# Two sets of operand sums moved beside an mLSTM head, half a plain tile put inside the last head, and weights split one half ahead

## The chip, the cores and the metric

The kernel runs on one core of a Trainium2 chip. The metric is the device time of one execution in microseconds. The median of three timed runs of the kernel before is 2468.99 us (2468.9 to 2470.32).

## The reference

One inference step of a hybrid layer: an in-projection, an mLSTM branch and a sliding-window attention branch side by side, two branch projections that are gated and added, an out-projection and a layer norm. The prompt has 512 tokens, the decode batch 8 x 4 = 32 samples; the model width is 2048.

```python
q_m, k_m, v_m, o_m, z_m, q_a, k_a, v_a, z_a, g_m, g_a, i_pre, f_pre = parts   # of x @ w_in
# prompt and samples, with their own states:
h_m, C, n, m = _mlstm(q, k, v, ig, lf, C0, n0, m0)       # 4 heads of 512
h_a = _sink_attend(q, k, v, dist, valid, slopes, sinks)  # window of 128, 32 heads of 64
# merge:
br_m = hn.reshape(B, T, M_WIDTH) * jax.nn.sigmoid(o_m) * jax.nn.silu(z_m)
br_a = h_a * jax.nn.silu(z_a)
y = (jax.nn.sigmoid(g_m) * jnp.einsum('btc,cd->btd', br_m, w_proj_m)
     + jax.nn.sigmoid(g_a) * jnp.einsum('btc,cd->btd', br_a, w_proj_a))
out = jnp.einsum('btc,cd->btd', y, w_out)
return _layernorm(DN_ALPHA * x + out, ln_w, ln_b).astype(x.dtype)
```

## The kernel before

All activations are held transposed: 128 channels on the partitions, the 544 tokens (512 of the prompt, 32 samples) as columns, in two halves of 272. Column 240 on, up to 272, is called the rim in the code of the sample attention.

Every fp32 value is split into a high and a low part (`split` for weights, `hilo` for activations), and a product is three matmuls: high with high, high with low, low with high. Half a weight tile is 128 x 8 x 128 values (`raw`); ScalarE casts it to `wh` (L208), VectorE forms `wl` (L209), TensorE multiplies (L218 for a plain tile, L693 and L695 for paired ones). A plain tile is two halves of 48 matmuls of 272 columns. Pairs of tiles are computed with seven half products instead of eight, from sums of the operand's four quarters, called s1, n2, n3 and s4: four VectorE operations on a row k and row k + 8 together, and a high and a low part of each.

The program runs in stages on TensorE: the in-projection in pairs, up to about 1760 us, with the prompt's attention, the sample attention (about 890 to 1011 us) and the samples' mLSTM worked in between the products; then the prompt's four mLSTM heads (1765 to 1984 us) with plain tiles of w_proj_a (numbers 0 to 5) worked in between; plain tiles 6 and 7 and the pairs of w_proj_a; plain tiles 14 and 15; four plain tiles of w_proj_m (2085 to 2134 us), its pairs, w_out, and the layer norm.

A scheduler sets the order of each engine. The code gives it generators that are advanced between products (`spawn`, `tick`, `yield`), priorities (`high_priority`), and pins (`issue_after(x)`: not ahead of instruction x). Each engine and each DMA queue takes its instructions strictly in the order so set. SP's queue carries most loads and stores, POOL's the loads of tile `tx`.

Names that the change touches:

- `d_bra[k]` is row k of the attention branch, 128 x 544. `attention` stores `hT` into it when head pair k is done; from row 8 on it loaded row k - 8 into `s`, formed the sums (`branch_sums`) and stored them in `d_sa[k - 8]`.
- `sample_attention` leaves the samples' columns in `gas`, stores them to `d_bra`, loads the rim of all rows into a part of `kb` (the tile of the samples' keys), formed the sums of the rim there and stored them in `d_ss`. The samples' mLSTM follows on SP's queue: loads of its state `C`, its `qs`, `ks`, `vs`; then `kA`, `qcl` go through memory (`d_kv`) and come back as `KB` and `VB`.
- `mlstm` runs the prompt's heads: `values`, `keys`, then `cells` (four cells c a head; L1485 is the key cell's matmul, L1533 the last group of matmuls of a cell).
- `plain_a(ct, ...)` is a plain tile of w_proj_a; its evacuation to `c` is L1694.
- `operand_sums(src, to, p)` loads rows k and k + 8 into `tx` (two buffers in this stage), forms the sums and splits them; row k + 2 is loaded when the sums of row k are done.
- `gemm` is a plain tile of two halves; `merged` evacuates a tile of w_proj_m (L1759) and adds the gated other half (L1760).

Of the kernel before, what the change touches and what calls it, by code (L numbers as in the profile page):

```python
# [74 lines left out]
def _build(tc, nc, i, o, es):  # L75
# [154 lines left out]
        return [bank(), bank()]  # L230

    def gemm(wv, c0, xh, xl, cols=EVEN, raws=(None, None), every=8, prio=0, before=None, parts=(1, 1),
             ps=None, behind=None):
        ps = ps or mm()
        for half in range(2):
            if before:
                before(half)
            raw = raws[half] or load_half(wv, c0, half)
            if prio:
                with tc.high_priority(offset=prio):  # L240
                    wh, wl = split(raw, parts=parts[half])
            else:
                with tc.issue_after(behind.ins) if behind and half == 0 else ExitStack():
                    wh, wl = split(raw, parts=parts[half])
            products(ps, half, wh, wl, xh, xl, cols, every[half] if isinstance(every, tuple) else every)
        return ps

    def halves(ps, ap, r=ALL):
# [541 lines left out]
    def attention(k, qs, sz, kv):  # L790


        k1, k2, VA = kv
        hT = btile("b1", [128, SEQ], "hT")
        st = []
        for a in range(2):
            nb = btile("b1", [128, 256], "nb")
            A.activation(nb[:], state["ca"][:, 0:256], AF.Copy, scale=SLOPES[2 * k + a])
            s_ = scores_tile()
            mx, mn, sums = (btile("bm", [128, 4], t_) for t_ in ("mx", "mn", "sums"))  # L800
            h = slice(2 * k + a, 2 * k + a + 1)
# [12 lines left out]
        yield  # L814
        for a in range(2):
            s_, mx, mn, sums, h = st[a]
            for j in range(4):
                sj = s_[:, j, 128 if j == 0 else 0:256]
                A.activation(sj, sj, AF.Exp, bias=mn[:, j:j + 1], scale=-1.0, accum_out=sums[:, j:j + 1])
            G.tensor_tensor(out=s_[:, 1:4, 128:256], in0=s_[:, 1:4, 0:128], in1=s_[:, 1:4, 128:256], op=ALU.add)  # L820
            A.activation(mx[:], mn[:], AF.Exp, bias=sinkb[:, h])
            V.tensor_tensor(out=sums[:], in0=sums[:], in1=mx[:], op=ALU.add)
            V.reciprocal(sums[:], sums[:])
            for j in range(4):
                sj = s_[:, j, 128:256]
                A.activation(sj, sj, AF.Copy, scale=sums[:, j:j + 1])
            yield
        yield
        ps_ = []
        for a in range(2):  # L830
            s_ = st[a][0]
            pt = sm()
            for b in range(4):
                PE.transpose(pt[:, b * 128:b * 128 + 128], s_[:, b, 128:256], ident)  # L834
            fh, fl = s_[:, :, 0:128], s_[:, :, 128:256]
            A.copy(fh.bitcast(F32R), blk(pt[:]))
            V.tensor_tensor(out=fl.bitcast(F32R), in0=blk(pt[:]), in1=fh, op=ALU.subtract)
# [12 lines left out]
        if k > 7:  # L850
            sc = scores_tile()
            nc.sync.dma_start(sc[:, 0:4:2, 0:PC], d_bra[k - 8].rearrange("p (c x) -> p c x", c=2)[:, :, 0:PC])
        for a in range(2):
            yield
            po = sm()
            for b in range(4):
                n = 256 if b < 3 else 128
                for m, p_ in enumerate(ps_[a]):
                    PE.matmul(po[:, b * 128:b * 128 + n], VA[:, b], p_[:, 2 * b:2 * b + n // 128],  # L859
                              start=(b == 0 and m == 0), stop=(b == 3 and m == 1), skip_group_check=True)  # L860
            rows_ = slice(a * 64, a * 64 + 64)
# [6 lines left out]
        if k > 7:  # L868
            spawn(branch_sums(sc[:, :, 0:PC], hT[:, 0:PC], hT[:, HT:SEQ], d_sa[k - 8]))

    PC = SEQ - HT

    def branch_sums(t_, r12, r22, to):
        r11, s1, r21, s4 = (t_[:, j] for j in range(4))
# [3 lines left out]
        V.tensor_tensor(out=s4, in0=r12, in1=r11, op=ALU.subtract)  # L878
        nc.sync.dma_start(to, t_)
        yield  # L880

    waiting = {}
    state.update(open=False, done=0, samples=False)
# [71 lines left out]
    def sample_attention():  # L955
# [119 lines left out]
        left = kb[:].rearrange("p b x -> p (b x)")  # L1075
        rim = left[:, 1024:1536].rearrange("p (k t) -> p k t", k=16)
        with tc.issue_after(state["load"].ins):
            nc.sync.dma_start(rim, d_bra[:, :, PC:HT].rearrange("k p t -> p k t"))
        PTs = weightsT(0)
        before = iter(())  # L1080
        for b2_ in range(4):
# [7 lines left out]
        for _ in before:  # L1089
            yield  # L1090
        nc.sync.dma_start(d_bra[:, :, SEQ:T].rearrange("k p t -> p k t"), gas[:])
        t_ = left[:, 0:1024].rearrange("p (j k t) -> p j k t", j=4, k=8)
        V.tensor_copy(t_[:, 0], rim[:, 0:8])
        V.tensor_copy(t_[:, 2], gas[:, 0:8])
        for _ in branch_sums(t_, rim[:, 8:16], gas[:, 8:16], d_ss):
            pass

    def layernorm_rows(n, den, em, parts, hn, w):

# [369 lines left out]
    def keys(h, c, kt):  # L1469
# [12 lines left out]
        for b in range(4):  # L1482
            for n, (a, b_) in enumerate(((kwh, vh), (kwh, vl), (kwl, vh))):
                for f, pp in enumerate((p0, p1)):
                    state["cells"] = PE.matmul(pp[:, 0:258], a[:, b * 128:b * 128 + 128], b_[:, b, f],  # L1485
                              start=(b == 0 and n == 0), stop=(b == 3 and n == 2))
        co = f5()
        A.copy(co[:, 0:256], p0[:, 0:256])
        A.copy(co[:, 256:512], p1[:, 0:256])
# [70 lines left out]
    def mlstm():  # L1560
# [3 lines left out]
        pre["k"] = load4(d_k, 0)  # L1564
        yield
        for h in range(MH):
            vts, kts = pre["v"], pre["k"]
            state["head"] = state["pow"]
            spawn(decays(h))
# [41 lines left out]

    wm, wa_, wo = kview("w_proj_m"), kview("w_proj_a"), kview("w_out")
    spawn(mlstm())
    def operand_sums(src, to, p, far=2):

        def load(k):
            t_ = tx.tile([128, 2, T], F32, tag="tx", name=nm("tx"))
# [4 lines left out]
        for k in range(8):  # L1622
# [4 lines left out]
            V.tensor_tensor(out=r22, in0=r22, in1=r21, op=ALU.subtract)  # L1627
            V.scalar_tensor_tensor(r21, r11, -1.0, r21, op0=ALU.mult, op1=ALU.subtract)
            V.tensor_tensor(out=r11, in0=r11, in1=r22, op=ALU.subtract)
            V.tensor_tensor(out=r12, in0=r12, in1=r11, op=ALU.subtract)  # L1630
            for name, r_ in (("s1", r22), ("n2", r11), ("n3", r21), ("s4", r12)):
                if name not in to:
                    to[name] = quad(p, name)
                hilo(r_, to[name][0][:, k], to[name][1][:, k])
            if k + far < 8:
                ahead.append(load(k + far))

# [93 lines left out]
    next(sums_)  # L1731
    spawn(sums_)
    for ct in range(LEAD_A, PAIR_A):
        with tc.issue_after(state["cells"].ins):
            plain_a(ct, every=2, prio=AHEAD)
    esPS.close()
    psB, psA = psum_pools(4)
    XA = operands((bah_, bal_), SA)
# [24 lines left out]


    M = {}
    spawn(operand_sums(d_brm, M, act))
    for ct in range(4):
        merge = merged(ct, plain=True)
        sg = merge([p_[:, :HT] for p_ in gemm(wm, ct * 128, bmh, bml, every=4, prio=AHEAD)])
        nc.sync.dma_start(d_y[ct], sg[:])  # L1770
    drain()
    XM = operands(bm_, M)

# [349 lines left out]
```

## Time and profile before

| what | value |
|---|---|
| median of the timed runs | 2468.99 us |
| time of the profiled execution | 2472.84 us |
| its span, first to last instruction | 2471.1 us |
| mean granted TensorE clock | 0.996 |
| TensorE (PE) busy | 2443.2 us, 99% |
| VectorE (DVE) busy | 1903.9 us, 77% |
| ScalarE (ACT) busy | 1247.9 us, 50% |
| GpSimd (POOL) busy | 523.2 us, 21% |

A row of a group or of the timeline names the line of the kernel, the engine, the operation, the tiles (written, then read), and the shape. In the timeline the first two numbers are start and length in us, and the bracket at the end is the idle time of the engine just ahead and what ended it. In a window's row stand its length, then busy time and number of instructions of PE, PE's weight loads, DVE, ACT and POOL, then the granted clock, the mean share of the DMA engines and GB/s. SPq and POOLq are the DMA-issuing queues of SP and POOL.

### The profile page before, as it was taken

The page shows a single profiled execution, that of the slowest core. Times are in us where ns is not written, and L with a number is a line of the kernel's source. Part 1 is how long each engine was busy: PE and PEld are TensorE (multiplying, and loading weights), DVE is VectorE, ACT ScalarE, POOL GpSimd, SP SyncE. Part 2 cuts the span into 40 slices and gives each one's busy share as a digit, 9 for nine tenths or more (in the row PEclk, how much of TensorE's full clock was granted, in tenths as well). Part 3 has the DMA queues.
Part 4 walks back from the last instruction along what each step waited for, and adds up shares of the span by engine and source line. Part 5 has one row for each costly group of instructions (what it writes and reads, how often), then busy time and mean ns, then how long its engine had stood idle before and what let it go on. Part 6 is the DMA issues. An engine that isn't in the chain of part 4 may idle for free.

```text
span 2471.1 us, 48979 instructions
## 1 busy us (share of the span) xinstructions
PE 2443.2 (99%) x19394; PEld 2379.0 (96%) x19394; DVE 1903.9 (77%) x2857; ACT 1247.9 (50%) x2069; POOL 523.2 (21%) x504
## 2 busy tenths in 40 slices
PE   9999999999999999999999999999999999999999
PEld 8999999999999998989999999999999999999997
DVE  7768888888888887877877888777855676777656
ACT  6466676676676654433433444444644444434431
POOL 4114334333334320211111121211000120111111
PEclk9999999999999999999999999999999999999999
DMA  6876666666776754577687676676754598788776
GB/s 180 201 176 159 156 160 148 161 161 165 172 181 165 174 155 120 157 218 226 194 251 233 174 237 209 192 233 214 245 162 156 183 254 259 217 228 268 203 221 186
DMA packets 566846, 479.03 MB, mean 194 GB/s; under 512 B 46424, under 2 KB 461704, under 8 KB 566360
## 3 DMA queue, kind: packets, MB, share of 16 engines
q1 hardware_dynamic: 547864, 410.09, 56.2%
q0 software_dynamic: 17840, 64.23, 13.3%
q8 instruction: 153, 2.51, 0.4%
q10 hardware_dynamic: 912, 1.57, 0.2%
q14 instruction: 77, 0.63, 0.1%
HBM read 325.75 MB, written 100.77 MB: 173 GB/s over the span
## 4 chain that ended last, share of the span: by engine, by line
PE 91%; issue 3%; DMA 3%; DVE 2%; ACT 0%; SPq 0%; POOL 0%; ACTq 0%; DVEq 0%; POOLq 0%
PE bank L693 46%; PE bank L695 23%; PE bank L218 8%; PE sm L1485 2%; PE sm L218 1%; PE sm L1517 1%; PE sm L808 1%; PE bank L1292 1%; PE sm L1533 1%; PE sm L859 1%; DVE wl L209 1%; PE sm L1944 1%; PE sm L1297 1%; DMA VB<-d_kv 1%; PE sm L834 1%
## 5 line engine op out<-in xcount | busy, mean ns | idle before, releaser
L208 ACT CAST wh<-raw 128x1024 fp32r<-128x1024 f32 x641 | 671.5, 1048 | 834.7 <-PE bank L693 707.6
L209 DVE TENSOR_TENSOR wl<-raw,wh 128x1024 fp32r<-128x1024 f32 x641 | 801.1, 1251 | 204.8 <-ACT wh L208 183.3
L693 PE MATMUL bank<-xk,wh 128*128 128x272 f32 x2336 | 323.7, 289 | 0.2 <-ACT wh L208 0.2
L673 DVE TENSOR_TENSOR raw<-raw,raw 128x1024 f32<-128x1024 f32 x244 | 309.9, 1271 | 7.8 <-issue 2.5
L693 PEld LDWEIGHTS bank<-xk,wh 128*128 128x128 f32 x2336 | 303.2, 188 | 2.4 <-issue 1.5
L712 POOL TENSOR_TENSOR ev<-p,ev 128x272 f32<-128x272 f32 x85 | 114.3, 1345 | 461.6 <-ACT ev L711 419.3
L693 PE MATMUL bank<-n3h,wh 128*128 128x272 f32 x656 | 170.7, 292 | 1.0 <-ACT ev L716 0.6
L693 PE MATMUL bank<-n2h,wh 128*128 128x272 f32 x656 | 170.0, 291 | 0.0
L693 PE MATMUL bank<-s1h,wh 128*128 128x272 f32 x656 | 169.8, 291 | 0.0
L695 PE MATMUL bank<-xk,wl 128*128 128x272 f32 x1168 | 169.5, 287 | 0.0
L693 PE MATMUL bank<-n3l,wh 128*128 128x272 f32 x656 | 168.9, 289 | 0.0
L693 PE MATMUL bank<-n2l,wh 128*128 128x272 f32 x656 | 167.9, 287 | 0.0
L693 PE MATMUL bank<-s4h,wh 128*128 128x272 f32 x656 | 167.5, 289 | 0.0
L693 PE MATMUL bank<-s1l,wh 128*128 128x272 f32 x656 | 167.4, 287 | 0.0
L693 PE MATMUL bank<-s4l,wh 128*128 128x272 f32 x656 | 167.0, 287 | 0.0
L695 PEld LDWEIGHTS bank<-xk,wl 128*128 128x128 f32 x1168 | 155.5, 188 | 0.1
L671 POOL DMA_DIRECT2D raw<-raw x96 | 83.5, 870 | 323.9 <-DVE ev L720 209.5
L693 PE MATMUL bank<-a11h,wh 128*128 128x272 f32 x584 | 150.4, 289 | 0.0
L693 PE MATMUL bank<-a11l,wh 128*128 128x272 f32 x584 | 149.6, 288 | 0.0
L693 PEld LDWEIGHTS bank<-n3h,wh 128*128 128x128 f32 x656 | 124.5, 190 | 2.8 <-issue 1.5
L693 PEld LDWEIGHTS bank<-s1h,wh 128*128 128x128 f32 x656 | 123.2, 188 | 1.6 <-issue 1.0
L693 PEld LDWEIGHTS bank<-n2h,wh 128*128 128x128 f32 x656 | 123.3, 188 | 1.5 <-issue 1.4
(529 smaller groups left out, 5806.6 us busy)
## 6 DMA issues: line engine op xcount, KB each, us to landing
raw<-in_w_in SPq DMA_DIRECT2D x296, 512.0 KB
raw<-raw POOLq DMA_DIRECT2D x96, 512.0 KB, 5.1
C<-in_state_mlstm_C SPq DMA_DIRECT2D x32, 1024.0 KB
out<-C SPq DMA_DIRECT2D x64, 512.0 KB
raw<-in_w_proj_a SPq DMA_DIRECT2D x32, 512.0 KB
raw<-in_w_proj_m SPq DMA_DIRECT2D x32, 512.0 KB
raw<-in_w_out SPq DMA_DIRECT2D x32, 512.0 KB
d_v<-ev SPq DMA_DIRECT2D x16, 272.0 KB
```

The source lines that it names most:

```text
L208: state["cast"] = A.copy(wh[:, k:k + n], raw[:, k:k + n])
L209: state["split"] = V.tensor_tensor(out=wl[:, k:k + n], in0=raw[:, k:k + n], in1=r32(wh[:, k:k + n]), op=ALU.subtract)
L218: PE.matmul(ps[f][:, :w], a[:, kk], b(k, c, w), start=(k == 0 and n == 0), stop=(k == 15 and n == 2))
L671: G.dma_start(out=w[out][:], in_=w[b][:], accum_op=ALU.add)
L673: V.tensor_tensor(out=w[out][:], in0=w[a][:], in1=w[b][:], op=ALU.add)
L693: PE.matmul(ps, wh[:, k], x(p, k), start=(first and k == 0 and p == 0), stop=False, skip_group_check=True)
L695: state["end"] = PE.matmul(ps, wl[:, k], x(0, k), start=False, stop=(k == 7), skip_group_check=True)
L712: G.tensor_tensor(out=c22, in0=p1, in1=c11, op=ALU.subtract)
L808: PE.matmul(pp[:, c0 + w0:c0 + 256], qs[a][:, j * 128:j * 128 + 128], kx[:, k0:k0 + 256 - w0], start=(n == 0), stop=(n == 1))
L834: PE.transpose(pt[:, b * 128:b * 128 + 128], s_[:, b, 128:256], ident)
L859: PE.matmul(po[:, b * 128:b * 128 + n], VA[:, b], p_[:, 2 * b:2 * b + n // 128], start=(b == 0 and m == 0), stop=(b == 3 and m == 1), skip ...
L1485: state["cells"] = PE.matmul(pp[:, 0:258], a[:, b * 128:b * 128 + 128], b_[:, b, f], start=(b == 0 and n == 0), stop=(b == 3 and n == 2))
```

## The change

Four things are changed.

1. Row 15 of the attention branch no longer forms the sums with row 7, and the sample attention no longer forms those of the rim. A new generator, `last_sums`, does both. It is spawned at the start of the second head: it loads rows 7 and 15 and then the two rims, forms four sums each, and stores them in eight pieces.
2. The first half of plain tile 6 is pinned behind the key cell of c = 1 of the last head, and no longer behind that head's last cell.
3. The four plain tiles of w_proj_m are made by `lead`, which loads and splits the weights of the next half ahead of the products of this one.
4. The operand sums of that stage are pinned behind the last split and the last cast that stand ahead of them in the code.

The four lines of the sums are now a function, `four_sums` (L875 to L878).

```diff
-        if k > 7:
+        if 7 < k < 15:
             spawn(branch_sums(sc[:, :, 0:PC], hT[:, 0:PC], hT[:, HT:SEQ], d_sa[k - 8]))
+    def last_sums():
+        def store(pairs):
+            with tc.issue_after(state["load"].ins):
+                for to, src in pairs:
+                    nc.sync.dma_start(to, src)
+        p_, q_ = ev(), ev()
+        with tc.issue_after(state["load"].ins):
+            for t_, k in ((p_, 7), (q_, 15)):
+                nc.sync.dma_start(t_[:, 0:SEQ], d_bra[k][:, 0:SEQ])
+        for _ in range(4):
+            yield
+        (r11, r21), (r12, r22) = ((t_[:, 0:PC], t_[:, HT:SEQ]) for t_ in (p_, q_))
+        with tc.issue_after(state["split"].ins):
+            four_sums(r11, r12, r21, r22, r22, r12)
+        yield
+        store([(d_sa[7][:, j], r_) for j, r_ in enumerate((r11, r22, r21, r12))])
+        a_, b_ = (ev()[:, 0:16 * NS].rearrange("p (k t) -> p k t", k=16) for _ in range(2))
...
+        with tc.issue_after(state["split"].ins):
+            four_sums(r11, r12, r21, r22, r22, r12)
+        yield
+        store([(d_ss[:, j], r_) for j, r_ in enumerate((r11, r22, r21, r12))])
...
-        with tc.issue_after(state["load"].ins):
-            nc.sync.dma_start(rim, d_bra[:, :, PC:HT].rearrange("k p t -> p k t"))
...
-        for _ in branch_sums(t_, rim[:, 8:16], gas[:, 8:16], d_ss):
-            pass
...
+        if c == 1:
+            state["keyed"] = state["cells"]
...
         for h in range(MH):
+            if h == 1:
+                spawn(last_sums())
...
+    def lead(wv, cts, xh, xl, every):
+        nxt = []
+        def prepare_half(ct, half):
+            raw = load_half(wv, ct * 128, half)
+            with tc.high_priority(offset=AHEAD):
+                nxt.append(split(raw))
+        todo = [(ct, half) for ct in cts for half in range(2)]
+        prepare_half(*todo[0])
+        for n, (ct, half) in enumerate(todo):
+            if n + 1 < len(todo):
+                prepare_half(*todo[n + 1])
...
+            products(ps, half, *nxt.pop(0), xh, xl, EVEN, every)
...
+            with behind("split"), behind("cast"):
+                four_sums(r11, r12, r21, r22, r22, r12)
+                for name, r_ in (("s1", r22), ("n2", r11), ("n3", r21), ("s4", r12)):
+                    hilo(r_, to[name][0][:, k], to[name][1][:, k])
...
-        with tc.issue_after(state["cells"].ins):
-            plain_a(ct, every=2, prio=AHEAD)
+        plain_a(ct, every=2, prio=AHEAD, pins=(state["keyed" if ct == LEAD_A else "cells"], state["cells"]))
...
-    spawn(operand_sums(d_brm, M, act))
+    spawn(operand_sums(d_brm, M, act, pinned=True))
```

How the order moves is shown at three places. The line numbers of the new kernel differ from the old by 1 to 52.

SP's queue at the end of the sample attention, before. `d_ss<-kb` is the store of the rim's sums, `C` and `qs`, `ks`, `vs` the first loads of the samples' mLSTM.

```order
L1091 DMA d_bra<-gas 128x16x32
L664 DMA raw_1667_12811<-in_w_in 128x8x128
L879 DMA d_ss<-kb 128x1024
L1346 DMA d_g<-ev_12388 128x544
L1151 DMA C_12534<-in_state_mlstm_C 128x4x512
L1159 DMA qs_12536<-d_q 128x4x32
L1159 DMA ks_12537<-d_k 128x4x32
L1159 DMA vs_12538<-d_v 128x4x32
```

The same place now:

```order
L1121 DMA d_bra<-gas 128x16x32
L1176 DMA C_12519<-in_state_mlstm_C 128x4x512
L1184 DMA qs_12521<-d_q 128x4x32
L1184 DMA ks_12522<-d_k 128x4x32
L1184 DMA vs_12523<-d_v 128x4x32
L1187 DMA w_12527<-in_state_mlstm_n 8x512
L1263 DMA gs_14562<-d_g 128x4x32
```

The loads of the state and of q, k, v now stand right behind the store of the samples' columns; the store of the rim's sums, a weight load and `d_g` no longer stand between. On PE the first matmul on `qs` stands 118 products behind the last one of the sample attention, before 203; the first matmul on `VB` stands 140 products behind the one on `qcl`, before 43.

SP's queue in the second head, now. `ev_21939` and `ev_21940` hold rows 7 and 15, `ev_22177` the second rim; `t` are the next head's loads. Before, the four `t<-d_k` followed the weight load at once.

```order
L195 DMA raw_22922<-in_w_proj_a 128x8x128
L891 DMA d_sa<-ev_21940 128x240
L891 DMA d_sa<-ev_21939 128x240 x2
L891 DMA d_sa<-ev_21940 128x240
L907 DMA ev_22177<-d_bra 128x16x32
L1583 DMA t_21880<-d_k 128x512
```

On DVE in the same head, now; L1745 is the evacuation of a bank of a plain tile, L875 to L878 the sums of the rim:

```order
L1136 TENSOR_TENSOR lns_21865<-lns_21865 128x1
L1137 SCALAR_TENSOR_TENSOR lns_21865<-lns_21865 128x1
L875 TENSOR_TENSOR ev_22177<-ev_22177 128x256
L876 SCALAR_TENSOR_TENSOR ev_22177<-ev_22176,ev_22177 128x256
L877 TENSOR_TENSOR ev_22176<-ev_22176,ev_22177 128x256
L1745 TENSOR_TENSOR c_2876_21521<-bank_21523,c_2876_21521 128x272
L878 TENSOR_TENSOR ev_22176<-ev_22176 128x256
L1745 TENSOR_TENSOR c_2876_21521<-bank_21524,c_2876_21521 128x272
```

Four stores and a load stand ahead of the next head's loads on SP, and three of the rim's sums ahead of the evacuation on DVE, where before it followed the small steps directly.

POOL's queue at the end of the plain tiles of w_proj_m, before. The `tx` are the loads of rows 4 to 7 for the operand sums, `raw` belongs to the paired stage.

```order
L1618 DMA tx_25536<-d_brm 128x2x544
L1618 DMA tx_25614<-d_brm 128x2x544
L1618 DMA tx_25682<-d_brm 128x2x544
L1618 DMA tx_25760<-d_brm 128x2x544
L671 DMA raw_25870<-raw_3485_25872 128x1024
```

And now:

```order
L1670 DMA tx_25551<-d_brm 128x2x544
L1670 DMA tx_25629<-d_brm 128x2x544
L1670 DMA tx_25697<-d_brm 128x2x544
L672 DMA raw_25879<-raw_3488_25881 128x1024
L1670 DMA tx_25775<-d_brm 128x2x544
```

DVE at the same place, now; L1809 and L1810 evacuate the last plain tile, `tx_25775` is row 7:

```order
L1809 TENSOR_TENSOR c_3483_25735<-bank_25734,c_3483_25735 128x272
L209 TENSOR_TENSOR wl_25892<-raw_3492_25889,wh_25891 128x1024
L1810 TENSOR_TENSOR c_3483_25735<-c_3483_25735,ev_25736 128x544
L875 TENSOR_TENSOR tx_25775<-tx_25775 128x272
L209 TENSOR_TENSOR wl_25898<-raw_25877,wh_25897 128x1024
L876 SCALAR_TENSOR_TENSOR tx_25775<-tx_25775 128x272
L255 TENSOR_TENSOR s1l_25386<-tx_25775,s1h_25385 128x272
```

Row 7 is now loaded behind a load of the paired stage, and its sums stand behind the evacuation of the last plain tile with splits of the paired stage among them; before they stood ahead of that evacuation. On PE the matmuls on s1 of row 7 have moved from the end of the s1 products behind fourteen products on n2, 52 products from the start of the paired stage.

More of the change, by code (lines that the diff above doesn't have):

```diff
@@ L232, in gemm @@
     def gemm(wv, c0, xh, xl, cols=EVEN, raws=(None, None), every=8, prio=0, before=None, parts=(1, 1),
-             ps=None, behind=None):
+             ps=None, behind=None, pins=(None, None)):
         ps = ps or mm()
@@ L244, in gemm @@
                     wh, wl = split(raw, parts=parts[half])
-            products(ps, half, wh, wl, xh, xl, cols, every[half] if isinstance(every, tuple) else every)
+            with tc.issue_after(pins[half].ins) if pins[half] else ExitStack():
+                products(ps, half, wh, wl, xh, xl, cols, every[half] if isinstance(every, tuple) else every)
         return ps
@@ L867, in attention, with four_sums @@
         nc.sync.dma_start(d_bra[k][:, 0:SEQ], hT[:])
-        if k > 7:
+        if 7 < k < 15:
             spawn(branch_sums(sc[:, :, 0:PC], hT[:, 0:PC], hT[:, HT:SEQ], d_sa[k - 8]))
     PC = SEQ - HT
-    def branch_sums(t_, r12, r22, to):
-        r11, s1, r21, s4 = (t_[:, j] for j in range(4))
+    def four_sums(r11, r12, r21, r22, s1, s4):
         V.tensor_tensor(out=s1, in0=r22, in1=r21, op=ALU.subtract)
@@ L878, in branch_sums @@
         V.tensor_tensor(out=s4, in0=r12, in1=r11, op=ALU.subtract)
+    def branch_sums(t_, r12, r22, to):
+        r11, s1, r21, s4 = (t_[:, j] for j in range(4))
+        four_sums(r11, r12, r21, r22, s1, s4)
         nc.sync.dma_start(to, t_)
         yield
+    def last_sums():
[15 more added lines that the diff above has]
+        a_, b_ = (ev()[:, 0:16 * NS].rearrange("p (k t) -> p k t", k=16) for _ in range(2))
+        with tc.issue_after(state["load"].ins):
+            nc.sync.dma_start(a_, d_bra[:, :, PC:HT].rearrange("k p t -> p k t"))
+            nc.sync.dma_start(b_, d_bra[:, :, SEQ:T].rearrange("k p t -> p k t"))
+        for _ in range(4):
+            yield
+        (r11, r12), (r21, r22) = ((t_[:, 0:8], t_[:, 8:16]) for t_ in (a_, b_))
+        with tc.issue_after(state["split"].ins):
+            four_sums(r11, r12, r21, r22, r22, r12)
+        yield
+        store([(d_ss[:, j], r_) for j, r_ in enumerate((r11, r22, r21, r12))])
     waiting = {}
@@ L1073, in values_of @@
                     V.tensor_tensor(out=gv, in0=src[:, :, a], in1=gv, op=ALU.mult)
-        left = kb[:].rearrange("p b x -> p (b x)")
-        rim = left[:, 1024:1536].rearrange("p (k t) -> p k t", k=16)
-        with tc.issue_after(state["load"].ins):
-            nc.sync.dma_start(rim, d_bra[:, :, PC:HT].rearrange("k p t -> p k t"))
         PTs = weightsT(0)
@@ L1091, in sample_attention @@
         nc.sync.dma_start(d_bra[:, :, SEQ:T].rearrange("k p t -> p k t"), gas[:])
-        t_ = left[:, 0:1024].rearrange("p (j k t) -> p j k t", j=4, k=8)
-        V.tensor_copy(t_[:, 0], rim[:, 0:8])
-        V.tensor_copy(t_[:, 2], gas[:, 0:8])
-        for _ in branch_sums(t_, rim[:, 8:16], gas[:, 8:16], d_ss):
-            pass
     def layernorm_rows(n, den, em, parts, hn, w):
@@ L1613, in _build, with operand_sums, behind @@
     spawn(mlstm())
-    def operand_sums(src, to, p, far=2):
+    def lead(wv, cts, xh, xl, every):
[9 more added lines that the diff above has]
+                prepare_half(*todo[n + 1])
+            if half == 0:
+                ps = mm()
+                yield ct, None
+            products(ps, half, *nxt.pop(0), xh, xl, EVEN, every)
+            if half:
+                yield ct, ps
+    def operand_sums(src, to, p, far=2, pinned=False):
+        def behind(name):
+            return tc.issue_after(state[name].ins) if pinned else ExitStack()
         def load(k):
@@ L1626, in operand_sums @@
             r11, r21, r12, r22 = (t_[:, a, c:c + HT] for a in range(2) for c in (0, HT))
[L1627 to L1631, printed above, removed]
+            for name in ("s1", "n2", "n3", "s4"):
                 if name not in to:
                     to[name] = quad(p, name)
-                hilo(r_, to[name][0][:, k], to[name][1][:, k])
+            with behind("split"), behind("cast"):
+                four_sums(r11, r12, r21, r22, r22, r12)
+                for name, r_ in (("s1", r22), ("n2", r11), ("n3", r21), ("s4", r12)):
+                    hilo(r_, to[name][0][:, k], to[name][1][:, k])
             if k + far < 8:
@@ L1765, in _build @@
     M = {}
-    spawn(operand_sums(d_brm, M, act))
[L1767 to L1770, printed above, removed]
+    spawn(operand_sums(d_brm, M, act, pinned=True))
+    for ct, ps in lead(wm, range(4), bmh, bml, 4):
+        if ps is None:
+            merge = merged(ct, plain=True)
+        else:
+            sg = merge([p_[:, :HT] for p_ in ps])
+            nc.sync.dma_start(d_y[ct], sg[:])
     drain()
```

## The prediction

> **What bounds the kernel now.** I read the page first, for the engine that carries the end.
>
> ```profile
> PE 2443.2 (99%) x19394; PEld 2379.0 (96%) x19394; DVE 1903.9 (77%) x2857; ACT 1247.9 (50%) x2069; POOL 523.2 (21%) x504
> PE 91%; issue 3%; DMA 3%; DVE 2%; ACT 0%; SPq 0%; POOL 0%; ACTq 0%; DVEq 0%; POOLq 0%
> tx<-d_brm POOLq DMA_DIRECT2D x8, 544.0 KB, 6.4
> ```
>
> TensorE is busy for all but some 28 us of the span and is 91% of the chain that ended last. The change removes no product; it can only win idle time of PE, or time at a lower granted clock. So the list of PE's waits came next.
>
> ```profile
> PE sm L1297 <- DMA VB<-d_kv: 5.7, 2, 3.3
> PE sm L1485 <- issue: 3.5, 1, 3.5
> PE bank L218 <- DVE wl L209: 1.4, 2, 1.2
> PE sm L1533 <- ACT t L1116: 0.9, 1, 0.9
> ```
>
> Each line is engine and line, what it waited for, total, times, longest. The edits reach the first VB wait (3.3), the t of L1116, both wl waits and three smaller ones shown below; the 3.5 us in front of L1485 lies in a place whose order is untouched. The windows give the clock behind long waits and the rate of an undisturbed stretch.
>
> ```profile
> 2000.00:2050.00 50.00, 50.00 (x400) 49.92 (x400) 36.19 (x48) 22.90 (x31) 9.62 (x10) 1.00 0.88 232
> 1054.60:1060.60 6.00, 6.00 (x27) 5.56 (x28) 2.72 (x4) 1.04 (x1) 0.10 (x1) 0.51 1.07 314
> 1592.00:1598.00 6.00, 6.00 (x50) 6.00 (x49) 5.04 (x7) 2.50 (x3) 0.00 (x0) 1.00 0.58 164
> 1784.00:1787.40 3.40, 3.40 (x17) 3.40 (x18) 3.40 (x6) 1.84 (x3) 0.00 (x0) 0.52 0.25 90
> ```
>
> 400 matmuls in 50 us is 0.125 us a product. The last number but two is the granted clock: behind the 3.3 us wait PE ran at 0.51 for 6 us (27 matmuls where 48 fit), behind the 3.5 us wait at 0.52 for 3.4 us, behind the other VB wait, which ended at 1592, at 1.00. So the wait at 1054 cost 3.27 us and then 6.0 x 0.49 = 2.9 us more.
>
> **Part 1: branch row 15 and the rim leave the sample attention.** The chain of waits (start, length, piece) and the issues of SP show what stood there.
>
> ```profile
> 1018.79 2.62 DMA d_ss<-kb
> 1021.94 0.46 SPq L1159
> 1044.42 3.08 DMA d_kv<-qcl
> 1047.64 6.81 DMA VB<-d_kv
> 1008.67 0.37 SPq L1091 DMA_DIRECT2D d_bra<-gas  x1
> 1031.46 0.97 PE L1171 MATMUL sm<-qs,rep 128*128 128x32 f32 x8
> 1043.00 0.42 PE L1212 MATMUL sm<-nT,qs 128*32 128x8 f32 x8 [0.86 <-DVE nT L1208]
> 1044.54 0.39 PE L1225 MATMUL sm<-qcl,Pst 128*32 128x512 f32 x1 [0.62 <-DVE qcl L1199]
> 1054.59 0.88 PE L1297 MATMUL sm<-VB,Ab 32*128 32x512 f32 x4 [3.27 <-DMA VB<-d_kv]
> ```
>
> The qs load stood behind the rim's store (1018.79) and its landing, 13.3 us after the gas store (1008.67). Without that store it follows the gas store at once. In the new order PE comes to the first matmul on qs after 118 products from the last one of the sample attention, before after 203: 85 x 0.125 = 10.6 us earlier, so qs is not the late one. Between the qcl matmul and the one on VB stand 140 products (17.5 us), before 43 (5.4 us); the store and the load together took 3.08 + 6.81 = 9.9 us. VB is then there 7 us early, also because its load no longer stands behind a second 1 MB load of C. So 3.27 and the 2.9 of the clock go. For nT and qcl 53 products (6.6 us) now lie between L1171's place and nT's; DVE has four splits and sums of 1.2 us there besides its small steps, which makes some 7.5 us against PE's 8.7: both waits (1.5 us together) go, or stay. I take 0.3 us left of all: 0.86 + 0.62 + 3.27 + 2.9 - 0.3 = **-7.4 us** (-7.7 to -6.1).
>
> The same edit brings the load of the sample attention's keys forward.
>
> ```profile
> 912.12 0.37 SPq L664 DMA_DIRECT2D raw<-in_w_in  x1
> 916.98 0.54 SPq L879 DMA_DIRECT2D d_sa<-s  x1
> 920.98 0.42 SPq L970 DMA_DIRECT2D kb<-in_state_attn_k  x1
> 928.95 0.52 PE L994 MATMUL sm<-cc,kb 128*128 128x128 f32 x3 [1.72 <-DMA kb<-in_state_attn_k]
> ```
>
> The load took 8.0 us from issue to use. In the new order it follows the 912.12 load with two short ones between, so about 914, landing 922; PE's transposes stand 52 products (6.5 us) earlier, at 920.7. Wait 1.3 instead of 1.7: I take **0** (-1.7 to +1.5).
>
> **Part 2: the sums in the second head.** Eight DVE operations, four loads' worth of traffic and eight stores come in. The second set stands ahead of the evacuation of a bank:
>
> ```profile
> 1816.93 1.23 DVE L209 TENSOR_TENSOR wl<-raw,wh 128x1024 fp32r<-128x1024 f32 x1
> 1826.75 0.79 DVE L1694 TENSOR_TENSOR c<-bank,c 128x272 f32<-128x272 f32 x2 [1.78 <-PE bank L218]
> 1827.36 0.37 PE L218 MATMUL bank<-bh,wh 128*128 128x272 f32 x1
> 950.85 0.53 SPq L1078 DMA_DIRECT2D kb<-d_bra  x1
> 955.47 0.29 DVE L1093 COPY kb<-kb 128x256 f32<-128x256 f32 x1
> 1818.66 1.96 SPq L1556 DMA_DIRECT2D t<-d_k  x4
> ```
>
> DVE sat idle for 1.78 us before that evacuation, and PE takes the bank up 0.6 us after it. The rim load reuses a buffer that two d_sa stores must have left. The first sums stand behind the split at 1816.93, so four operations and two small steps later they end about 1820; the stores of that buffer go at 1819.8 and land some 2.6 us later (d_ss above), and the load at 1822.4 takes up to 4.6 us (950.85 to its first reader at 955.47): there at 1826 to 1827. Then three operations of 0.4 us, the two evacuations with the fourth between: PE gets its bank some 0.8 us late, **+0.8 us** (0 when the load takes 3 us, 3 when the stores land late). The four t<-d_k loads behind it on SP go 4.7 us later than at 1818.66, at 1823.4 to 1825; the transposes on them come at 1830, so they hide.
>
> **Part 3: the half plain tile in the last head.**
>
> ```profile
> 1952.06 0.39 PE L1485 MATMUL sm<-vh,kwh 128*128 128x258 f32 x1 [0.16 <-ACT kwh L253]
> 1968.07 0.39 PE L1533 MATMUL sm<-vh,ph 128*128 128x258 f32 x1 [0.86 <-ACT t L1116]
> ```
>
> 48 products (6 us) that stood behind the head now lie inside it, 20 of them behind the key cell, 25 ahead of the last group of L1533. They fill both waits: **-1.0 us** (-1.0 to 0).
>
> **Part 4: weights split ahead, operand sums pinned behind the splits.**
>
> ```profile
> 2104.76 0.39 PE L218 MATMUL bank<-bh,wl 128*128 128x272 f32 x1 [1.21 <-DVE wl L209]
> 2117.26 0.39 PE L218 MATMUL bank<-bh,wl 128*128 128x272 f32 x1 [0.20 <-DVE wl L209]
> 2097.63 0.44 DVE L1627 TENSOR_TENSOR tx<-tx 128x272 f32<-128x272 f32 x1 [4.51 <-DMA tx<-d_brm]
> 2118.84 0.72 POOL L1618 DMA_DIRECT2D tx<-d_brm  x1 [6.75 <-DVE s4l L254]
> 2135.02 2.00 PE bank L693 x16
> L209 DVE TENSOR_TENSOR wl<-raw,wh 128x1024 fp32r<-128x1024 f32 x9 | 11.0, 1219 | 2.5 <-ACT wh L208 2.5
> DMA to landing us min/median/max: 4.2/6.8/7.9
> ```
>
> DVE waited 4.51 us for a load of tx with a split queued behind it; that is the 1.21. With the split ahead both go: -1.4 us. But the sums now start later: none before about 2093, and the load of row k+2 is issued when sum k is done. The paired products start at 2134.9, less 1.4 = 2133.5; half tiles of 48 products lie 6.0 us apart before that. Sum 4 stands behind the split of the half that starts at 2121.5, done about 2117.0; its eight DVE operations at 0.4 us or less end at 2120.2. The load of row 6 lands 6.4 us later (the page's median), 2126.6; sums 5 and 6 run interleaved with a split among them and end about 2133.0; the load of row 7, before issued at 2118.84, lands at 2139.4. Ahead of s1's low part then stand on DVE the subtraction, a split of 1.2 us and two more: 2141.8. PE comes to that product 52 products behind 2133.5, at 2140.0. New wait 1.8, and some 0.1 for n2 behind it: +1.9, so **+0.5 us** in all. With loads of 4.2 us there is no wait (-1.4); with 7.9 us the wait is 4.9 (+3.5, and a clock dip).
>
> The Trainium skill, "DMA: Bandwidth & Descriptors", section "Issuing engines are not separate DMA queues", says that transfers of SP and POOL interleave on the same 16 engines. The spread of 4.2 to 7.9 us agrees; by that rule the load of row 7, which goes out among the raw loads of the paired stage, would be nearer 7.9, and the sum 3 us worse.
>
> **Sum.** -7.4 + 0 + 0.8 - 1.0 + 0.5 = -7.1 us against the profiled execution's 2472.84. That one is 3.85 above the median of the timed runs, 2468.99; I take the difference over to the median: **2461.9 us**, -0.29%. A measurement of this kernel can tell about 0.2%, 4.9 us.
>
> **Rivals.** *The clock dip at 1054 is not in the timed runs.* The dip lengths differ (6.0 and 3.4 us) for waits of like length, and the 3.85 us would fit one run with and the others without. Then 2.9 us less is won: 2464.8, within the bound. Against it: each wait over 3 us in this trace has its dip. The Trainium skill, "TensorE: Matmul & The Clock Gate", Part 1, says that the clock falls to half after an idle window of about 3.4 us and that this window runs free. By that rule a wait of 3.27 us should not have dipped, and did here, so the measurement decides; a free phase would let other executions of the same kernel go without.
>
> *Row 7 comes late and PE falls into a dip.* Loads of 7.9 us throughout: wait 4.9 in place of 1.9 and 2.9 for the clock, net -7.1 + 5.9 = -1.2: 2467.8. For it, two loads of the row took over 7 us; against it, one took 4.2. It decides from a row-7 landing after 2140.9, where the wait passes 3.3.
>
> *Slower: the key load doesn't move up.* If it still goes at 921 because a wait of SP ahead of it holds it, PE, 6.5 us earlier at L994, waits 8.2 in place of 1.7 and dips (2.9): +9.4, net +2.3: 2471.3. It decides from an issue at about 919. Against it: of the instructions ahead of it only the hT store (911.04 in the queue before) remains, the d_sa store and a weight load are gone. With row 7 late too it would pass the bound.
>
> *The change doesn't do what it says*: the order shows each move, so this has no chance of its own.
>
> **How the numbers follow.** Forecast 0.63, no dip in the timed runs 0.16, row 7 late 0.13, key load late 0.05, others 0.03. Best terms: -7.7 - 1.7 - 1.0 - 1.4 = -11.8, all at once unlikely; I go down to -11: 2458.0. Upward the range takes in both middle rivals: 2468.5. Faster: nearly all of the forecast's 0.63 and a little of the first rival; within 0.2%: the two rivals and the forecast's edge; slower: half of the last rival and the unforeseen.
>
> **What would show it.** Right: no wait over 1 us between 1000 and 1064 on PE and clock 1.00 there; the two wl waits gone; a wait of s1's products at the start of the paired w_proj_m of 1 to 3 us; about 1 us at the evacuation in the second head; the waits for t of L1116 gone. Wrong: a wait over 3 us at L994, in the second head or at row 7, above all with a clock of 0.5 behind it; or a before whose timed runs lack the dip.

## The result, and the profile after

The changed kernel takes 2462.06 us (median of six, 2460.19 to 2465.63). The kernel before, with three more runs beside it, takes 2471.36 us (2468.9 to 2473.71). The ratio is 0.9964, with a 95% interval of 0.9951 to 0.9977: 8.9 us less (5.7 to 12.1). The forecast was 2461.9 us and a gain of 7.1. That the time came within 0.2 us is luck in part: the forecast started from the first three runs of before, whose median (2468.99) lies 2.4 us under that of all six, and the medians now lie 9.3 us apart, 2.2 more than forecast. The profiled execution took 2462.88 us.

The page after, with busy time and number of instructions of each engine:

```profile
span 2460.9 us, 48990 instructions
PE 2438.6 (99%) x19394; PEld 2376.6 (97%) x19394; DVE 1903.9 (77%) x2855; ACT 1249.5 (51%) x2069; POOL 522.0 (21%) x504
```

The longest of PE's waits after (total, times, longest; two at the program's start, of 3.3 and 3.0 us, are left out, they were 3.3 and 2.1):

```profile
PE bank L218 <- DVE c L1745: 4.1, 2, 2.8
PE sm L1510 <- issue: 3.5, 1, 3.5
PE sm L1322 <- DMA VB<-d_kv: 1.5, 1, 1.5
PE bank L694 <- ACT wh L208: 1.2, 2, 1.0
PE sm L1028 <- DMA kb<-in_state_attn_k: 0.5, 1, 0.5
```

The first VB wait, nT, qcl, the t wait of the last head and both wl waits are gone. At the top stands a wait that hardly existed: the evacuation of a bank, 4.1 us in two pieces. The 1.5 us for VB is the second unit's, near 1580 us, where nothing was changed.

As PE runs 19394 matmuls in both, one can ask how much earlier or later the n-th of them starts. Working that out for every 600th shows where the time went. At places that the change touches: -7.7 us between 970 and 1130 us and -1.8 ahead of it in the sample attention, **+3.0** in the second head, **+0.5** from there to the pairs of w_proj_a, -1.9 in the plain tiles of w_proj_m; together -7.9. At places where PE's order is the same: +1.2 at the program's start (its first loads), -0.4 at about 1380 us, -1.0 at the second unit's VB, and some -2 in the stages behind w_proj_m's plain tiles; together -2.2. These are not shown to be the change's doing. Nearly all of the last one lies in the layer norm: the last 94 matmuls and what follows took 27.7 us in place of 30.2, and in a second execution of the kernel before, 26.2.

The place of part 1, in the windows after:

```profile
1040.00:1064.00 24.00, 24.00 (x193) 22.78 (x192) 19.30 (x21) 10.22 (x14) 6.37 (x7) 1.00 0.67 206
```

And in the timeline after, SP's issues and PE:

```profile
1008.03 0.37 SPq L1121 DMA_DIRECT2D d_bra<-gas  x1
1012.26 0.37 SPq L1184 DMA_DIRECT2D qs<-d_q  x1
1033.11 0.54 SPq L1171 DMA_DIRECT2D VB<-d_kv  x1
1048.93 0.50 PE L1322 MATMUL sm<-VB,Ab 32*128 32x512 f32 x4
```

PE is busy throughout and its clock is 1.00. The qs load goes 4.2 us behind the gas store, before it was 13.3, and VB's load is issued 15.8 us ahead of its use, before 6.95.

The new wait in the second head (SP's issues, DVE, PE):

```profile
1808.97 2.06 SPq L891 DMA_DIRECT2D d_sa<-ev  x4
1815.46 0.37 SPq L907 DMA_DIRECT2D ev<-d_bra  x1
1818.97 0.43 DVE L875 TENSOR_TENSOR ev<-ev 128x256 f32<-128x256 f32 x1 [3.69 <-DMA ev<-d_bra]
1820.72 0.39 PE L218 MATMUL bank<-bh,wh 128*128 128x272 f32 x1 [2.80 <-DVE c L1745]
```

The last of the four stores left SP at 1811.03. The rim's load, which reuses a buffer of theirs, could go only at 1815.46. DVE stood still for 3.69 us in front of the first sum, and the evacuation stood behind the sums.

The end of the last head and the start of the pairs of w_proj_a (PE, and ScalarE ahead of the second wait):

```profile
1978.14 0.39 PE L218 MATMUL bank<-bh,wh 128*128 128x272 f32 x1 [1.34 <-DVE c L1745]
2000.48 0.39 PE L694 MATMUL bank<-bh,wh 128*128 128x272 f32 x1 [1.05 <-ACT wh L208]
1997.63 0.59 ACT L254 CAST sumh<-ev 128x480 fp32r<-128x480 f32 x1 [1.04 <-DMA ev<-d_sa]
1999.39 1.03 ACT L208 CAST wh<-raw 128x1024 fp32r<-128x1024 f32 x1
```

The bank's wait there was 0.50 us before. The second wait is new: ScalarE takes its instructions in order, and the weight cast stands behind casts of operand sums whose loads were late.

The end of the plain tiles of w_proj_m (POOL, DVE, PE):

```profile
2126.90 0.72 POOL L1670 DMA_DIRECT2D tx<-d_brm  x1 [6.83 <-DVE s4l L255]
2131.01 0.45 DVE L875 TENSOR_TENSOR tx<-tx 128x272 f32<-128x272 f32 x1 [0.45 <-DMA tx<-d_brm]
2132.86 0.43 DVE L255 TENSOR_TENSOR s1l<-tx,s1h 128x272 fp32r<-128x272 f32 x1
2133.35 0.39 PE L694 MATMUL bank<-s1l,wh 128*128 128x272 f32 x1
```

Row 7 landed 4.1 us behind its issue. Its low part of s1 was written at 2133.29, and PE used it at 2133.35: no wait, by 0.06 us.

### The profile page after: what moved, and what is told of

Read it like the earlier page. It is cut to its first block, busy times and chain, and to the rows that moved or that the text cites. A ratio compares the mean times of both kernels' runs of the same rounds, so it can differ in the third digit from the quotient of the medians.

```text
span 2460.9 us, 48990 instructions
## 1 busy us (share of the span) xinstructions
PE 2438.6 (99%) x19394; PEld 2376.6 (97%) x19394; DVE 1903.9 (77%) x2855; ACT 1249.5 (51%) x2069; POOL 522.0 (21%) x504
## 4 chain that ended last, share of the span: by engine, by line
PE 95%; DMA 2%; DVE 1%; ACT 0%; issue 0%; SPq 0%; POOL 0%; DVEq 0%; POOLq 0%; ACTq 0%
PE bank L694 48%; PE bank L696 23%; PE bank L218 10%; PE sm L1510 2%; PE sm L218 1%; PE bank L1317 1%; PE sm L1544 1%; PE sm L809 1%; PE sm L860 1%; PE sm L1560 1%; PE sm L1996 1%; PE sm L835 1%; PE sm L1322 1%; DMA ev<-d_sa 0%; PE bank L418 0%
## 5 line engine op out<-in xcount | busy, mean ns | idle before, releaser
L674 DVE TENSOR_TENSOR raw<-raw,raw 128x1024 f32<-128x1024 f32 x244 | 309.7, 1270 | 10.4 <-DMA raw<-in_w_in 3.0
L694 PEld LDWEIGHTS bank<-s4h,wh 128*128 128x128 f32 x656 | 123.2, 188 | 1.6 <-issue 1.4
```

Source lines behind the costliest of these rows:

```text
L674: V.tensor_tensor(out=w[out][:], in0=w[a][:], in1=w[b][:], op=ALU.add)
L694: PE.matmul(ps, wh[:, k], x(p, k), start=(first and k == 0 and p == 0), stop=False, skip_group_check=True)
```

## The experiments

The theories after this result. By the traces: part 1 won 7.7 us of waits and clock and 1.2 at the key load, part 2 cost 2.8 through the rim's load, part 3 cost 0.9, part 4 won 1.4; in all -6.6. The rival is the prediction's own list: -7.4, 0, +0.8, -1.0, +0.5. Its sum, -7.1, is as good.

**The kernel before against itself.**

> The kernel before, unchanged, as its own comparison: ratio 1.000. Theory of the traces: the dips of the granted clock belong to the waits of over 3 us, so this profile again has a wait of about 3.3 us for VB near 1054 us and a clock of 0.5 behind it, and a mean clock of 0.996. Rival (free window): the dip at 1054 is missing in this execution while the wait is there, the mean clock is 0.997 or more, and the time lies some 3 us lower.

Ratio 1.0002 (0.9993 to 1.0011). PE's waits near 1050 us:

```profile
PE sm L1297 <- DMA VB<-d_kv: 4.0, 1, 4.0
PE sm L1212 <- DVE nT L1208: 0.7, 1, 0.7
PE sm L1225 <- DVE qcl L1199: 0.6, 1, 0.6
```

The wait and its dip are there: the mean clock from 1050 to 1064 us is 0.76, as in the prediction's profile.

```profile
1050.00:1064.00 14.00, 10.00 (x60) 8.54 (x59) 5.74 (x9) 2.36 (x3) 1.72 (x5) 0.76 0.83 216
```

Every run also has a mean granted clock, and the 28 runs of before beside these four kernels sort by it: 2475.5 us at 0.995 (3 runs), 2472.9 at 0.996 (13), 2471.5 at 0.997 (9), 2468.3 at 0.998 (3). So about 2.4 us of difference between executions of one kernel go with each 0.001 of clock. The profiled execution of the prediction (0.996) was an ordinary one, and the three runs that it had beside it were on the low side.

**Parts 1 and 2 alone.**

```diff
+            if h == 1:
+                spawn(last_sums())
...
```

Both sums are gone from the sample attention, as in the change.

> Only the sums moved out of the sample attention into the second head (parts 1 and 2); plain tiles, splits and operand sums as before. Theory of the traces: the waits for nT, qcl and VB near 1040 to 1055 us and the dip go (-7.7 us), the key wait falls to about 0.5 us (-1.2), a wait of about 2.8 us for a bank's evacuation appears in the second head: -6.1 us, ratio 0.9975. The prediction's terms: -7.4, 0 and +0.8, so -6.6 us, ratio 0.9973, with a bank wait under 1 us. The two differ in the profile, not in the time.

Ratio 0.9968 (0.9956 to 0.998), 7.9 us less (4.9 to 10.9). Of PE's waits:

```profile
PE bank L218 <- DVE c L1720: 2.1, 2, 1.6
PE bank L218 <- DVE wl L209: 1.9, 2, 1.6
PE sm L1557 <- ACT t L1140: 0.9, 1, 0.9
```

Nothing waits between 900 and 1064 us. The bank wait in the second head is 1.6 us here (the other one, 0.5, stands behind the last head as before). That is above the predicted 0.8 and below the 2.8 of the traces: the rim's load was let go 3.1 us behind the last store's issue, not 4.4. The waits of parts 3 and 4 stand as before.

**Which of the two sums?** Only the rim moved, or only row 15.

```diff
...
+        a_, b_ = (ev()[:, 0:16 * NS].rearrange("p (k t) -> p k t", k=16) for _ in range(2))
...
+        p_, q_ = ev(), ev()
...
```

With the rim only, `last_sums` keeps the part that starts with the first line, and row 15 its `branch_sums`; with the row only it keeps the part that starts with the second, and the rim stays in the sample attention.

> Of parts 1 and 2 only the rim's sums are moved into the second head, with both loads at its start, each in a buffer of its own; row 15 keeps its sums where they were. Theory: the waits for nT, qcl and VB near 1040 to 1055 us stood behind the rim's store, so these go with the rim alone, the key wait of 1.7 us stays or grows by at most 1 us, and no bank wait appears: 4.8 us of waits and on average some 2 to 3 us of the clock, ratio about 0.997. Rival (row 15's sums delay the whole sample attention, and it is these that count): the VB wait stays above 2 us, ratio 0.999 or more.

> Of parts 1 and 2 only row 15's sums are moved into the second head; the rim stays in the sample attention. Theory: the key wait near 928 us falls from 1.7 to 0.5 us or none, the waits for nT, qcl and VB stay (4 to 5 us), no bank wait in the second head since no load waits for a store: -1.2 us, ratio 0.9995. Rival as above: VB's wait goes too, ratio 0.997.

Rim only: 0.9958 (0.9945 to 0.9972), 10.4 us less (6.9 to 13.6). Row only: 0.9986 (0.9976 to 0.9996), 3.5 us less (1.0 to 5.9). PE's waits from 900 to 1064 us, with the rim only:

```profile
PE sm L1016 <- DMA kb<-in_state_attn_k: 1.6, 1, 1.6
```

And with row 15 only:

```profile
PE sm L1319 <- DMA VB<-d_kv: 1.2, 1, 1.2
PE sm L1234 <- DVE nT L1230: 0.8, 1, 0.8
PE sm L1247 <- DVE qcl L1221: 0.6, 1, 0.6
PE sm L1016 <- DMA kb<-in_state_attn_k: 0.6, 1, 0.6
```

The rim's sums, with their load and store, held VB, nT and qcl; row 15 held the keys. The rim alone, in buffers of its own, has no bank wait in the second head, and its time can't be told from that of the whole change (0.9964).

VB's wait of 1.2 us with row 15 only looks as if row 15 had done more than expected. It is the dip that moved. The windows of that kernel, and of the kernel with part 3 alone, whose order at this place is that of before:

```profile
1040.00:1064.00 24.00, 21.42 (x161) 19.59 (x160) 19.09 (x29) 8.10 (x10) 8.51 (x11) 0.93 0.62 174
1043.00:1047.00 4.00, 3.58 (x16) 3.52 (x17) 3.58 (x7) 1.05 (x2) 3.60 (x3) 0.57 0.38 127
```

In both PE ran at half clock from about 1043 to 1047 us, came to VB later, and waited 1.2 and 2.1 us there. From the matmul on qcl to the one on VB it is 9.50 us with row 15 only and 10.05 in before, so what VB waits for comes only half a us sooner; the rest of the 2.1 us by which its wait is shorter went into the dip.

**Part 3 alone.**

```diff
-        with tc.issue_after(state["cells"].ins):
-            plain_a(ct, every=2, prio=AHEAD)
+        plain_a(ct, every=2, prio=AHEAD, pins=(state["keyed" if ct == LEAD_A else "cells"], state["cells"]))
```

> Only the half plain tile inside the last head (part 3). The prediction's term: both waits at 1952 and 1968 us filled, -1.0 us, ratio 0.9996. Theory of the traces: those two go (-1.0), but the head's end comes 6 us of products earlier, so the bank's evacuation behind the head's last four VectorE operations is waited for 1.3 us in place of 0.5, and at the start of the paired w_proj_a a weight cast stands behind the casts of late operand loads, 1 us: +0.9 us, ratio 1.0004.

Ratio 1.0006 (0.9998 to 1.0015): from 0.5 us less to 3.7 more, 1.5 more at the middle. The gain of 1.0 lies outside. PE at the two places:

```profile
1984.41 0.39 PE L218 MATMUL bank<-bh,wh 128*128 128x272 f32 x1 [1.34 <-DVE c L1697]
2006.34 0.39 PE L694 MATMUL bank<-bh,wh 128*128 128x272 f32 x1 [0.65 <-ACT wh L208]
```

The two fills are made (no wait at t, nor the one of 0.16 us at the key cell), and both new waits come with this part alone.

**Part 4 alone.**

```diff
+    spawn(operand_sums(d_brm, M, act, pinned=True))
+    for ct, ps in lead(wm, range(4), bmh, bml, 4):
...
```

> Only the weights split ahead and the operand sums pinned (part 4). Theory of the traces: the two waits for wl (1.4 us) go and no wait takes their place, since loads of tx land 4 to 5 us after their issue: -1.4 us, ratio 0.9994. The prediction's term: a wait of about 1.9 us for s1 of row 7 at the start of the paired w_proj_m: +0.5 us, ratio 1.0002.

Ratio 0.9993 (0.9984 to 1.0001): from 4.0 us less to 0.2 more, so the forecast's +0.5 lies just outside. PE waits for nothing between 2080 and 2150 us, and the loads of tx land in

```profile
DMA to landing us min/median/max: 4.0/4.9/6.8
```

**A buffer of its own for the second rim, or its sums later.** Both on the changed kernel.

```diff
-        a_, b_ = (ev()[:, 0:16 * NS].rearrange("p (k t) -> p k t", k=16) for _ in range(2))
+        a_, b_ = (t_[:, 0:16 * NS].rearrange("p (k t) -> p k t", k=16) for t_ in (ev(), rimp.tile([128, 512], F32, name="rim2")))
...
-        for _ in range(4):
+        for _ in range(8):
             yield
```

The first two lines are the one kernel, the eight yields ahead of the rim's sums the other.

> The changed kernel with a buffer of its own for the second rim, so that its load goes out at the start of the second head and waits for no store. Theory (the rim load waited for the landing of two stores of sums, 4.4 us behind the last store's issue, and the evacuation stood behind it): the bank wait in the second head, 1.6 to 2.8 us, falls to under 0.3 us, ratio to the kernel before about 0.9955. Rival (the wait is DVE's own time for three sums of 0.4 us ahead of the evacuation, or the eight stores crowd the queue): 0.8 us or more stays there or at the next head's loads, ratio 0.9963 or more.

> The changed kernel with eight yields in place of four ahead of the rim's sums, so that they stand behind the evacuation on VectorE; the load still waits for the stores. Theory: the bank wait in the second head goes as with a buffer of its own, ratio about 0.9955, but VectorE may stand a little at the sums and hold up what is behind them. Rival: the wait stays or moves to the transposes on the next head's keys, which are loaded 4 to 7 us later than before: 1 us or more there.

Own buffer: 0.9946 (0.9932 to 0.9959). Later: 0.9947 (0.9934 to 0.9961). With the own buffer PE waits for nothing from 1800 to 1900 us. Its rim load, among SP's issues:

```profile
1761.75 2.01 SPq L907 DMA_DIRECT2D rim<-d_bra  x1
```

With the later sums, the only wait of PE from 1800 to 1900 us:

```profile
PE sm L1510 <- ACT kwh L254: 0.5, 1, 0.5
```

With its own buffer the load goes 46 us ahead of the store of its first sum (1807.95), and the sums are done some 6 us before the evacuation; the eight stores are still there. With the later sums the load still waits for the stores, but the evacuation stands ahead of the sums. So the wait needed both, a load that the reuse of a buffer made late and an evacuation behind it on DVE. The three sums themselves took 1.3 us on DVE in the changed kernel, behind the 3.69 us that it stood still.

Both edits changed more than that. PE's order differs from that of the changed kernel between 1811 and 1979 us (at 1014 and 901 of the 19394 places), and behind the last cell of the last head stand 192 products of plain tiles, as in before, where the changed kernel has 144. The waits that came with part 3 are gone with that: for the bank behind the head PE waits 0.50 and 0.59 us, for the cast not at all. With its own buffer PE gains 3.1 us on the changed kernel at the second head and 1.9 from there to the pairs of w_proj_a. The intervals overlap that of the changed kernel (0.9951 to 0.9977), so it is the profile that tells these gains, not the time.

**The load of row 7 twice.**

```diff
+            if pinned and k == 7:
+                G.dma_start(out=t_[:], in_=src[k:k + 9:8].rearrange("k p t -> p k t"))
```

> The changed kernel with the load of row 7 for the operand sums of w_proj_m issued twice in a row into the same buffer (one load of 544 KB more). Theory of the forecast's part 4 (PE waits as soon as row 7 lands after about 2131 us on the changed kernel's clock; there it landed at 2131.0 and PE came to s1 of that row at 2133.2): a second load adds its 4 to 6 us, PE waits 4 to 6 us less some 0.1 at s1 of row 7, and if that passes about 3 us the clock may fall behind it (1 to 3 us more): ratio 0.998 to 0.9995. Rival (the sums of row 7 are not what PE waits for there; the forecast had the place wrong): no wait at s1, ratio 0.9964.

Ratio 0.9983 (0.9973 to 0.9992). PE at s1 of row 7, in the timeline:

```profile
2136.61 0.60 PE L694 MATMUL bank<-s1h,wh 128*128 128x272 f32 x1 [4.34 <-ACT s1h L254]
```

The window behind that wait:

```profile
2136.60:2143.00 6.40, 6.38 (x27) 6.20 (x28) 4.58 (x8) 3.57 (x6) 2.23 (x2) 0.50 0.05 10
```

The first load took 4.8 us; the second, which went out behind it, 5.9. That gives a wait of 4.34 us and then 6.4 us at half the clock. The place was right: PE waits there as soon as row 7 is late.

**Parts 1, 2 and 4 with the own buffer, without part 3.**

> Parts 1, 2 and 4 with a buffer of its own for the second rim, and without part 3 (the half plain tile). Theory: no bank wait in the second head, the t wait of 0.9 us near 1960 stays, the bank wait behind the last head is 0.5 us in place of 1.3, and the cast wait at the start of the paired w_proj_a goes: 0.9 us under the kernel with its own rim buffer, ratio about 0.9951. Rival (part 3 is worth its 1.0 us): 1.0 us over that kernel, ratio 0.9959.

2458.74 us, ratio 0.9943 (0.993 to 0.9955). It is the lowest, but the intervals of the own buffer (0.9946), the later sums and the rim only overlap it.

This run was meant to price part 3 a second time, and it can't. PE's 19394 matmuls stand in the same order here as with the own buffer and part 3, by line and tile: with the own buffer the scheduler leaves 192 products behind the last cell with the pin or without it, and products of plain tiles lie inside the head in both. They fill the wait for t, which had been expected to stay, and behind the head PE waits

```profile
PE bank L218 <- DVE c L1743: 0.5, 1, 0.5
```

as with the own buffer and part 3. What part 3 is worth is told by its own run alone.

## Why the prediction was right, and where it wasn't

*Part 1, -7.4.* Right, in size and place: the rim's sums were the cause, and all of 0.86, 0.62 and 3.27 went together with the clock behind them. The 0.3 left over was not needed. Their move set SP's loads and PE's matmuls in a new order at once (PE's at 196 places from 1017 to 1045 us), and no run has one without the other; so how much each did is not shown.

*The key load, 0.* Its issue came at 914.64, as worked out; it landed in 7.2 us in place of 8.0, and PE came 0.6 us later than worked out. The wait fell by 1.2 us, within the bounds given.

*The second head, +0.8.* The mechanism was right, the term mis-sized: 1.6 to 2.8 us. The step that failed is the landing of the stores, taken as 2.6 us from the one store of the rim; the load was let go 4.4 us behind the last store's issue, and 3.1 in parts 1 and 2 alone. The load itself took 3.5.

*The half tile, -1.0.* Wrong in sign. The fills were right; what failed is that the prediction did not ask what the moved products had hidden. Taking 6 us of products from behind the head leaves the evacuation and the operand loads behind it 6 us less to hide in: 0.84 us and 0.55 to 1.05 us. All runs agree with that: the three with 144 products behind the last cell (the changed kernel, part 3 alone, the load twice) wait 1.34 us for the bank and then for the cast, the nine with 192 wait 0.50 to 0.59 us for the bank and not for the cast. The bound of 0 on that side had no row behind it.

*Weights ahead and pinned sums, +0.5.* The 1.4 came; the new wait of 1.9 did not. The load of row 7 was issued 0.2 us behind the start of the paired stage, 0.7 later than worked out, but landed in 4.1 us and not in 6.4. With 6.4 the wait would have been about 2.2 (an estimate from these rows): the term hung on a duration of the kernel before. That the loads land faster because the pins set them apart is not shown. From the rule that SP's and POOL's transfers interleave (the Trainium skill, "DMA: Bandwidth & Descriptors", "Issuing engines are not separate DMA queues") the prediction had read a landing near 7.9 for this load. That reading failed by the measured 4.1; the rule itself says nothing of a time. (The 3 us that the prediction put on it also need row 6 at 7.9 us, 1.5 for each of the two.)

So the sum was right because +2.0 and +1.9 that were missed stood against -1.9 and -1.2 that were missed too. Of the rivals, row 7 late was real as a mechanism and missed by the landing alone; the slower one fell, as the key load did move up. The first, no dip in the timed runs, fell as far as the runs can tell: all four profiles with the waits of before at this place (before, control, parts 3 and 4 alone) show one there, with a mean clock of 0.76 to 0.88 from 1050 to 1064 us, and the timed runs' clocks fit that, before mostly at 0.995 to 0.997, the changed kernel at 0.997 to 0.999.

## What to carry to other kernels

When work is moved to where an engine has time, follow its buffers and not only its instructions: a load into a buffer that a store must leave first put a DMA round trip of 3.1 to 4.4 us in front of an in-order queue, and one more buffer took away a wait of 2.8 us, more than parts 3 and 4 won together. A tile that fills a wait inside a stage is taken from behind it, so look what it hid there. When an edit is meant to price one part, compare the engine's order with and without it first: two kernels that differ in the code can run the same order, as those with the own buffer did with part 3 and without. And check the terms one by one on the chip: a right total was made of two errors up and two down.

## What the runs showed of the hardware that I had not expected

How long PE waits does not tell whether its clock falls. The window behind a wait of 2.0 us, in parts 1 and 2 alone:

```profile
1578.50:1583.00 4.50, 4.45 (x24) 4.02 (x25) 3.69 (x5) 0.20 (x1) 0.76 (x1) 0.62 0.31 98
```

Behind one of 2.1 us, in part 3 alone:

```profile
1053.80:1058.00 4.20, 4.18 (x22) 3.76 (x23) 2.72 (x4) 0.00 (x0) 0.00 (x0) 0.60 1.02 270
```

Behind one of 2.8 us, in the last kernel above:

```profile
1580.20:1584.00 3.80, 3.75 (x30) 3.51 (x31) 3.22 (x5) 1.02 (x1) 0.78 (x1) 1.00 0.29 100
```

The two shorter waits were followed by a clock of about 0.6 over some 4 us, the longest by none; the 3.5 us wait in front of the key cell's matmul had a dip in each profile. The second unit's VB wait was 2.26 us with the rim only and 2.25 us with the later sums: the first was followed by a mean clock of 0.58 over 4.0 us, the second by 1.00. And the half clock from 1043 us with part 3 alone, shown above, came behind waits of 0.79 and 0.62 us only.

The Trainium skill, "TensorE: Matmul & The Clock Gate", Part 1, has the clock watched in windows of about 3.4 us that run free of the program. A free window would explain why like waits dip in one execution and not in another, and the prediction was too quick to set it aside; no run here shows the window itself. That waits well under one window are followed by a dip as well is more than an idle window of 3.4 us explains; why they are stays open.
